# A two-layer encoder trunk on one core: the first conv block's conditioning split into scale first and shift last

## The chip, the cores and the metric

The kernel runs on one core of one Trainium2 chip. The metric is the device time in microseconds, as the median of several runs.

## The reference

The model is a trunk of two layers over x of 1024 tokens by 1024 features, in float32. Each layer normalises, modulates by a conditioning vector, mixes, and ends with a squared-ReLU MLP; layer 0 mixes with a gated short convolution, layer 1 with latent attention. The part that matters here is the entry of layer 0:

```python
c_act = silu(c)
mod = c_act @ ada_w[0] + ada_b[0]            # (1, 6 * 1024)
sh_m, sc_m, g_m, sh_f, sc_f, g_f = split(mod, 6)
h = rmsnorm(x, norm_g[0, 0]) * (1 + sc_m) + sh_m
bcx = h @ conv_in_w                          # 1024 x 3072
b_gate, c_gate, xh = split(bcx, 3)
u = c_gate * xh
conv = depthwise_conv(u, w_conv, width 3, causal) + b_conv
y = (b_gate * conv) @ w_out
x = x + g_m * rmsnorm(y, norm_g[0, 1])
```

The columns of `ada_w[0]` that belong to the shift (0 to 1023) and the scale (1024 to 2047) are 8 MB together; x is 4 MB.

## The kernel before

Every float32 operand of a product is split into a high part (rounded to the type that TensorE takes at full speed) and a low part (the difference); `mm` issues three matmuls: low by high, high by low, high by high. On the way ScalarE writes the high part and VectorE the low one (`split_w` at L163 and L164 for weights).

`conv_phase` computes the first part of layer 0. It holds h transposed, in tiles of 128 features by 512 tokens: feature tile k (0 to 7) and token half (0 or 1). In turn it

- loads conditioning columns (`ada`, tile `aw`, three buffers): for each k, 128 columns of scale and 128 of shift over all 1024 rows, 1 MB in four transfers. `ada_end` forms the product with silu(c) as an accumulation on VectorE over eight row blocks (tile `av`, L821 and L823), sums over partitions by two small matmuls with ones (L825), and makes the scale and the shift (tile `sh`, L826 and L828);
- loads x (eight row tiles `y`), normalises it (`norm_x`: square with sum and root on ScalarE, L245 and L247, reciprocal and product on VectorE, L252 and L898);
- transposes on TensorE (`turn`, L833, four transposes for a tile), and scales and shifts at the eviction (`scaled`): ScalarE writes the high part and the full value (L839), VectorE the low part (L840);
- multiplies (`products`): for each (k, half) three groups g (the c gate, the b gate, xh) of three matmuls each, 512 columns, into six accumulators in PSUM. The first column block (m = 0) goes through the sixteen (k, half) as they become ready, half 1 two steps (`LAG`) behind half 0. Then `evict(0)`, and the second column block (m = 1) over the same h. Meanwhile `sums` (L888 to L894) forms sums and differences of the quarters of h, the operands of the following column blocks;
- goes on with the remaining column blocks in pairs (`all_pairs`), a scheme of seven products for eight.

The weights of one (k, m) are 128 by 384; their raw form goes through two buffers in turn (tags acc and gmb), the split forms through a ring of four (`wr`). The order of TensorE and of the transfer queue on SyncE is pinned as written in `conv_phase`; VectorE's and ScalarE's order is left to the scheduler when the program is built. The evictions' second half (`end` in `evict`: convolution, gate, store) runs later, among the pairs.

Of the kernel before, what the change touches and what calls it, by code (L numbers as in the profile page):

```python
# [17 lines left out]
P = 128  # L18
D = 1024
S = 1024  # L20
KD = D // P
# [16 lines left out]
LAG = 2  # L38
# [11 lines left out]
def trunk_kernel(ctx: ExitStack, tc: tile.TileContext, x, c, ada_w, ada_b, norm_g, conv_in_w, conv_w,  # L50
                 conv_b, conv_out_w, kv_ada_w, kv_ada_b, kv_norm_g, kv_a_w, kv_a_norm_g, kv_b_w,
                 q_a_w, q_a_norm_g, q_b_w, attn_o_w, mlp_up_w, mlp_down_w, consts, out):
    nc = tc.nc
    uid = [0]

    def nm(s):
        uid[0] += 1
        return f"{s}_{uid[0]}"
# [4 lines left out]
    cp = pool("cp")  # L63
# [21 lines left out]
    def tp_ps():  # L85
        return ps.tile([P, HALF], F32, tag="tp", name=nm("tp"))
# [10 lines left out]
    def row_tile():  # L97
        return yp.tile([P, D], F32, tag="y", name=nm("y"), bufs=NT)
# [15 lines left out]
    def ld(out_, in_):  # L114
        nc.sync.dma_start(out_, in_)
# [32 lines left out]
    bias = cp.tile([P, BIAS_ROWS], F32, name="bias")  # L148
# [306 lines left out]
    def halves(t):  # L455
        return t[:, :HALF], t[:, HALF:]
# [307 lines left out]
    w0, w1 = ada_w[0], ada_w[1]  # L764
    x0 = x[0]

    def conv(v, u, m, lo_, hi_):

        nc.scalar.activation(v[:, lo_:hi_], u[:, lo_:hi_], AF.Identity, scale=cw[2][:, m:m + 1], bias=cb[:, m:m + 1])
        for back in (1, 2):  # L770
            o = max(lo_, back)
            nc.vector.scalar_tensor_tensor(v[:, o:hi_], u[:, o - back:hi_ - back], cw[2 - back][:, m:m + 1], v[:, o:hi_],
                                           op0=ALU.mult, op1=ALU.add)

    def conv_phase():
# [4 lines left out]
        wr = pool("wr")  # L780
# [3 lines left out]
        ops = {n: as_quarter(t_) for n, t_ in zip(("11", "21", "22"), (s11, s21, slots_of(ca, 1)[0]))}  # L784
# [20 lines left out]
        nc.vector.tensor_scalar(g1, gain(0, 0), RMS, None, op0=ALU.mult)  # L805
        nc.vector.scalar_tensor_tensor(b1, bias[:, 8:16], 1.0, g1, op0=ALU.add, op1=ALU.mult)
        sh = [cp.tile([P, 2], F32, name=nm("sh")) for _ in range(KD)]

        def ada(k):
# [8 lines left out]
        def ada_end(k, raw):  # L818
            p_ = tp_ps()
            acc = st.tile([P, 2 * P], F32, tag="av", name=nm("av"), bufs=2)  # L820
            nc.vector.tensor_scalar(acc, raw[:, 0, :], csil[:, 0:1], None, op0=ALU.mult)  # L821
            for i in range(1, KD):
                nc.vector.scalar_tensor_tensor(acc, raw[:, i, :], csil[:, i:i + 1], acc, op0=ALU.mult, op1=ALU.add)  # L823
            for j in range(2):
                nc.tensor.matmul(p_[:, j:j + 1], acc[:, j * P:(j + 1) * P], ones[:, 0:1], start=True, stop=True)  # L825
            nc.vector.scalar_tensor_tensor(sh[k][:, 0:1], p_[:, 0:1], g1[:, k:k + 1], b1[:, k:k + 1], op0=ALU.mult,  # L826
                                           op1=ALU.add)
            nc.vector.tensor_tensor(sh[k][:, 1:2], p_[:, 1:2], bias[:, k:k + 1], op=ALU.add)  # L828

        def turn(k, half):  # L830
            p_ = tp_ps()
            for t in range(4):
                nc.tensor.transpose(p_[:, t * P:(t + 1) * P], xt[half * 4 + t][:, k * P:(k + 1) * P], ident)  # L833
            return p_

        def scaled(k, p_, dst, name):
            hi, lo = ops[name][k % 4]
            for out_ in (hi, dst):
                nc.scalar.activation(out_, p_, AF.Identity, scale=sh[k][:, 0:1], bias=sh[k][:, 1:2])  # L839
            nc.vector.tensor_tensor(lo, dst, hi.bitcast(F32), op=ALU.subtract)  # L840

        def old(k):
            return kept[k % 4][:, (k // 4) * HALF:(k // 4 + 1) * HALF]

        new = [None] * 4

        def weights(k, m):

            raw = ad.tile([P, D], F32, tag=("acc", "gmb")[k % 2], name=nm("w"), bufs=1)[:, :3 * P]
            ld(raw.rearrange("p (g m) -> p g m", g=3),  # L850
               conv_in_w[0][k * P:(k + 1) * P, :].rearrange("p (g c) -> p g c", g=3)[:, :, m * P:(m + 1) * P])
            w = [wr.tile([P, 3 * P], F32R, tag="w" + part_, name=nm("w"), bufs=4) for part_ in "hl"]
            split_w(w[0], w[1], raw)
            return w

# [7 lines left out]
        def evict(m, acc):  # L863
            b, c_, u, v = (row_tile() for _ in range(4))
            for half in range(2):
                sl = slice(half * HALF, (half + 1) * HALF)
                nc.scalar.activation(c_[:, sl], acc[1, half], AF.Copy)
                nc.scalar.activation(b[:, sl], acc[0, half], AF.Copy)
                nc.vector.tensor_tensor(u[:, sl], acc[2, half], c_[:, sl], op=ALU.mult)

            def end():
                conv(v, u, m, 0, S)
                nc.vector.tensor_tensor(v, v, b, op=ALU.mult)
                nc.scalar.dma_start(hd[m], v)

            late.append(end)
# [19 lines left out]
        def norm_x(half):  # L896
            for t in range(4 * half, 4 * half + 4):
                nc.vector.tensor_scalar(xt[t], xt[t], rroot(squares(nx, xt[t])), None, op0=ALU.mult)  # L898

        def first_half(k):  # L900
            raw = ada(k)
            if k == 0:
                load_x(0)
                norm_x(0)
            elif k == LAG:
                load_x(1)
            p_ = turn(k, 0)
            ada_end(k, raw)
            scaled(k, p_, old(k), ("11", "21")[k // 4])

        def second_half(k):
            if k < 4:
                new[k] = halves(raw_tile())
            scaled(k, turn(k, 1), new[k % 4][k // 4], ("12", "22")[k // 4])

        with pinned([mybir.EngineType.PE, mybir.EngineType.SP]):
            w = [weights(0, 0)]
            first_half(0)
            acc = banks6()
            for k in range(KD + LAG):  # L920
                if k < KD - 1:
                    w.append(weights(k + 1, 0))
                    first_half(k + 1)
                if k < KD:
                    products(w[k], k, 0, acc)
                if k == LAG:
                    norm_x(1)
                    second_half(0)
                if k >= LAG:
                    if k - LAG < KD - 1:  # L930
                        second_half(k - LAG + 1)
                    products(w[k - LAG], k - LAG, 1, acc)
                if k == KD:
                    w.append(weights(0, 1))
            w = w[KD]
            st.release()
            evict(0, acc)
            cB = pool("cB", "right")
            for n, t_ in zip(("t1", "t2"), slots_of(cB, 2)):
                ops[n] = as_quarter(t_)  # L940
            ops["t3"], ops["t4"] = [], {}
            acc = banks6()
            for k in range(KD):
                w, w_ = weights(k + 1, 1) if k < KD - 1 else None, w
                products(w_, k, 0, acc)
                products(w_, k, 1, acc)
                if k % 2 == 0:
                    sums(k // 2)
            evict(1, acc)
# [130 lines left out]
    def cols_of(w, n):  # L1080
# [5 lines left out]
    up, ws, hs, firsts, _ = down_phase(slots, (2, 2, 4), conv_out_w[0], from_dram(hd), "g0m", x0, xs[0],  # L1086
                                      mlp_up_w[0], "0f")
# [93 lines left out]
    steps = h_steps(tp, ys, 0, "kv", hk[0])  # L1181
# [3 lines left out]
    steps = h_steps(tp, ys, 1, "kv", hk[1])  # L1185
# [166 lines left out]
    for h in range(H):  # L1352
# [82 lines left out]
    up, ws, hs, firsts, _ = down_phase(slots, (2, 2, 4), attn_o_w[0], from_dram(hd), "g1m", xs[1], xs[2],  # L1435
                                      mlp_up_w[1], "1f")
# [52 lines left out]
```

## Time and profile before

| | us |
|---|---|
| median of 3 runs | 2187.67 |
| lowest and highest run | 2184.27, 2188.56 |
| profiled execution, span from first to last instruction | 2182.7 |
| profiled execution's own time beside the span | not shown |
| TensorE busy in the span | 2092.2 (96%) |
| VectorE busy | 1518.3 (70%) |
| ScalarE busy | 1065.2 (49%) |
| transferred | 329.90 MB |

Everything the change touches lies in the first 160 us or so. TensorE's share there is the place to look at; from about 85 us on it is busy throughout.

### The profile page before, as it was taken

The page shows a single profiled execution, that of the slowest core. Times are in us where ns is not written, and L with a number is a line of the kernel's source. Part 1 is how long each engine was busy: PE and PEld are TensorE (multiplying, and loading weights), DVE is VectorE, ACT ScalarE, POOL GpSimd, SP SyncE. Part 2 cuts the span into 40 slices and gives each one's busy share as a digit, 9 for nine tenths or more (in the row PEclk, how much of TensorE's full clock was granted, in tenths as well). Part 3 has the DMA queues.
Part 4 walks back from the last instruction along what each step waited for, and adds up shares of the span by engine and source line. Part 5 has one row for each costly group of instructions (what it writes and reads, how often), then busy time and mean ns, then how long its engine had stood idle before and what let it go on. Part 6 is the DMA issues. An engine that isn't in the chain of part 4 may idle for free.

```text
span 2182.7 us, 25276 instructions
## 1 busy us (share of the span) xinstructions
PE 2092.2 (96%) x9654; PEld 1717.5 (79%) x9654; DVE 1518.3 (70%) x2005; ACT 1065.2 (49%) x1513; POOL 4.0 (0%) x8
## 2 busy tenths in 40 slices
PE   4999999899999999999899999999899999999998
PEld 3788888688888778888677888878688887788886
DVE  6877776876555578956788776665866665558556
ACT  4533354754444433344665555564754444444342
POOL 0000000000000000000000000000000000000000
PEclk9999999999999999999999999999999999999999
DMA  8444463256443977444224131053255553853343
GB/s 229 117 138 139 139 221 124 76 174 207 164 159 126 331 255 252 164 146 173 77 69 132 55 113 44 30 170 112 75 165 179 183 179 124 307 195 126 97 145 135
DMA packets 240111, 329.90 MB, mean 151 GB/s; under 512 B 18581, under 2 KB 141810, under 8 KB 239990
## 3 DMA queue, kind: packets, MB, share of 16 engines
q1 hardware_dynamic: 202104, 247.25, 36.0%
q10 hardware_dynamic: 37886, 81.03, 9.8%
q8 instruction: 76, 1.25, 0.2%
q14 instruction: 45, 0.37, 0.1%
HBM read 247.50 MB, written 80.74 MB: 150 GB/s over the span
## 4 chain that ended last, share of the span: by engine, by line
PE 76%; DVE 12%; ACT 6%; DMA 4%; issue 2%; ACTq 0%; SPq 0%; DVEq 0%
PE one L160 40%; PE mm L160 19%; PE tp L160 7%; PE big L160 4%; PE big L1282 2%; ACT junk L245 2%; DVE y L302 2%; DVE raw L303 2%; DMA raw<-in_ada_w_dram 1%; PE tp L1308 1%; DVE acc L185 1%; DVE y L296 1%; DMA raw<-ha 1%; DVE small L1285 1%; ACT small L247 1%
## 5 line engine op out<-in xcount | busy, mean ns | idle before, releaser
L160 PE MATMUL one<-slot,uphi 128*128 128x512 f32 x1224 | 377.4, 389 | 0.0
L160 PE MATMUL big<-slot 128*128 128x512 f32 x1152 | 267.9, 392 | 0.6 <-DVE slot L164 0.4
L160 PEld LDWEIGHTS one<-slot,uphi 128*128 128x128 f32 x1224 | 230.1, 188 | 48.2 <-issue 0.5
L160 PEld LDWEIGHTS big<-slot 128*128 128x128 f32 x1152 | 216.0, 188 | 46.1 <-ACT y L746 1.0
L164 DVE TENSOR_TENSOR uplo<-raw,uphi 128x1024 fp32r<-128x1024 f32 x127 | 153.0, 1221 | 137.0 <-ACT uphi L163 136.9
L160 PE MATMUL one<-slot,uplo 128*128 128x512 f32 x612 | 240.3, 393 | 5.9 <-ACT y L564 2.3
L160 PE MATMUL one<-ring,ring 128*128 128x512 f32 x1008 | 233.6, 392 | 6.8 <-DVE ring L164 6.8
L163 ACT ACTIVATE ring<-w 128x1024 fp32r<-128x1024 f32 x98 | 103.7, 1059 | 262.9 <-PE tp L160 131.5
L160 PEld LDWEIGHTS one<-ring,ring 128*128 128x128 f32 x1008 | 189.5, 189 | 49.8 <-ACT ring L163 5.6
L163 ACT ACTIVATE uphi<-raw 128x1024 fp32r<-128x1024 f32 x127 | 134.5, 1061 | 128.6 <-PE one L160 88.7
L164 DVE TENSOR_TENSOR ring<-w,ring 128x1024 fp32r<-128x1024 f32 x98 | 119.7, 1221 | 109.7 <-ACT ring L163 109.6
L160 PE MATMUL mm<-slot,uphi 128*128 128x512 f32 x520 | 165.0, 398 | 9.7 <-DVE slot L363 9.3
L160 PE MATMUL mm<-ring,ring 128*128 128x512 f32 x672 | 162.4, 390 | 0.0
L160 PE MATMUL tp<-ring,ring 128*128 128x512 f32 x672 | 161.7, 389 | 0.0
L185 DVE SCALAR_TENSOR_TENSOR acc<-raw,csil,acc 128x1024 f32<-128x1024 f32 x88 | 112.8, 1281 | 49.8 <-DMA raw<-in_ada_w_dram 46.4
L160 PEld LDWEIGHTS mm<-ring,ring 128*128 128x128 f32 x672 | 125.7, 188 | 27.1 <-DVE ring L164 0.6
L160 PEld LDWEIGHTS tp<-ring,ring 128*128 128x128 f32 x672 | 126.2, 188 | 26.2
L160 PEld LDWEIGHTS one<-slot,uplo 128*128 128x128 f32 x612 | 115.1, 188 | 33.0 <-ACT y L489 3.7
L164 DVE TENSOR_TENSOR ring<-raw,ring 128x1024 fp32r<-128x1024 f32 x98 | 119.3, 1218 | 18.2 <-ACT ring L163 18.2
L160 PEld LDWEIGHTS mm<-slot,uphi 128*128 128x128 f32 x520 | 97.4, 189 | 33.3 <-DVE slot L363 10.8
L489 ACT ACTIVATE y<-one 128x512 f32<-128x512 f32 x66 | 39.0, 590 | 169.3 <-PE one L160 93.2
L160 PE MATMUL one<-slot,s 128*128 128x512 f32 x468 | 112.6, 389 | 0.5 <-DVE s L164 0.5
(255 smaller groups left out, 3474.4 us busy)
## 6 DMA issues: line engine op xcount, KB each, us to landing
ha<-y ACTq DMA_DIRECT2D x196, 256.0 KB, 3.9
raw<-ha SPq DMA_DIRECT2D x98, 512.0 KB, 3.9
raw<-in_ada_w_dram SPq DMA_DIRECT2D x80, 512.0 KB, 4.3
raw<-in_mlp_up_w_dram SPq DMA_DIRECT2D x70, 512.0 KB, 4.3
w<-in_mlp_down_w_dram SPq DMA_DIRECT2D x56, 512.0 KB, 5.3
raw<-hd SPq DMA_DIRECT2D x24, 512.0 KB, 4.5
xs<-raw ACTq DMA_DIRECT2D x24, 512.0 KB, 3.4
raw<-xs SPq DMA_DIRECT2D x24, 512.0 KB, 3.3
```

The source lines that it names most:

```text
L160: nc.tensor.matmul(out_, lhs[a], rhs[b], start=first and i == 0, stop=last and i == 2, skip_group_check=more)
L163: nc.scalar.activation(hi, src, AF.Copy)
L164: nc.vector.tensor_tensor(lo, src, hi.bitcast(F32), op=ALU.subtract)
L185: nc.vector.scalar_tensor_tensor(acc, raw, s, acc, op0=ALU.mult, op1=ALU.add)
L245: nc.scalar.activation(junk, src, AF.Square, accum_out=ss)
L247: nc.scalar.activation(rt, ss, AF.Sqrt, bias=eps_d)
L296: nc.vector.tensor_tensor(y, y, p_, op=ALU.add)
L302: nc.vector.scalar_tensor_tensor(y, y, rroot(ss), self.gmb, op0=ALU.mult, op1=ALU.mult)
L303: nc.vector.tensor_tensor(xr, xr, y, op=ALU.add)
L489: nc.scalar.activation(dst, x_, AF.Copy)
L1282: nc.tensor.matmul(o_, a, m_, start=j == 0, stop=j == 4 and b * HALF + w < n)
L1285: nc.vector.tensor_reduce(mx, sp[:, :n], AX.X, ALU.max, negate=True)
```

## The change

Scale and shift are loaded apart: `ada(col, q)` takes 256 columns of one of them, for the feature tiles 2q and 2q+1, in two transfers. The four scale tiles come first; the four shift tiles follow. `scaled` makes h without the shift, and the first column block (three feature tiles of the result: b, c and xh for m = 0) is computed from it. When a shift has come (`shift_end`), `shifted` adds it to the four h tiles in place: two ScalarE operations and one difference on VectorE for each. The shift's share in the first column block is computed by `bias_products`: for each k and group two matmuls (high and low weights) with the shift's high and low part as two columns, 48 in all, 36 after the first block and 12 after the first product pair of the second. The share (`add`, three numbers for each feature) is added in the later part of `evict`. The sixteen products of the first block follow a written list of steps; the ring of split weights has ten buffers instead of four, so that the first block's weights stay.

```diff
+        def ada(col, q):
             raw = st.tile([P, KD, 2 * P], F32, tag="aw", name=nm("aw"), bufs=3)
             for i in (0, 4):
-                for j, col in enumerate((D, 0)):
-                    ld(raw[:, i:i + 4, j * P:(j + 1) * P],
-                       w0[i * P:(i + 4) * P, col + k * P:col + (k + 1) * P].rearrange("(k p) m -> p k m", p=P))
+                ld(raw[:, i:i + 4, :],
+                   w0[i * P:(i + 4) * P, col + 2 * q * P:col + 2 * (q + 1) * P].rearrange("(k p) m -> p k m", p=P))
             return raw
...
+        def scale_end(q, raw):
+            pr = slice(2 * q, 2 * q + 2)
+            sc[q] = cp.tile([P, 2], F32, name=nm("sc"))
+            nc.vector.tensor_tensor(sc[q], ada_end(raw), g1[:, pr], op=ALU.mult)
+            nc.vector.tensor_tensor(sc[q], sc[q], b1[:, pr], op=ALU.add)
+
+        def shift_end(q, raw):
+            sh[q] = cp.tile([P, 2], F32, name=nm("sh"))
+            nc.vector.tensor_tensor(sh[q], ada_end(raw), bias[:, 2 * q:2 * q + 2], op=ALU.add)
+            shr[q] = cp.tile([P, 2, 2], F32R, name=nm("shr"))
+            nc.vector.tensor_copy(shr[q][:, :, 0], sh[q])
+            nc.vector.tensor_tensor(shr[q][:, :, 1], sh[q], shr[q][:, :, 0].bitcast(F32), op=ALU.subtract)
+            for half in range(2):
+                for k in (2 * q, 2 * q + 1):
+                    shifted(k, half)
...
+        def scaled(k, half, p_):
+            f, (hi, lo) = place(k, half)
+            for out_ in (hi, f):
+                nc.scalar.activation(out_, p_, AF.Copy, scale=sc[k // 2][:, k % 2:k % 2 + 1])
+            nc.vector.tensor_tensor(lo, f, hi.bitcast(F32), op=ALU.subtract)
+
+        def shifted(k, half):
+            f, (hi, lo) = place(k, half)
+            for out_ in (hi, f):
+                nc.scalar.activation(out_, f, AF.Identity, bias=sh[k // 2][:, k % 2:k % 2 + 1])
+            nc.vector.tensor_tensor(lo, f, hi.bitcast(F32), op=ALU.subtract)
...
-            w = [wr.tile([P, 3 * P], F32R, tag="w" + part_, name=nm("w"), bufs=4) for part_ in "hl"]
+            w = [wr.tile([P, 3 * P], F32R, tag="w" + part_, name=nm("w"), bufs=10) for part_ in "hl"]
...
+        def bias_products(ws_, ks, out_):
+            for k in ks:
+                for g in range(3):
+                    for q in ws_[k]:
+                        nc.tensor.matmul(out_[:, 2 * g:2 * g + 2], q[:, g * P:(g + 1) * P], shr[k // 2][:, k % 2, :],
+                                         start=k == 0 and g == 0 and q is ws_[k][0],
+                                         stop=k == KD - 1 and q is ws_[k][1], skip_group_check=True)
+
+        def evict(m, acc, add=None):
...
+                if add is None:
+                    nc.vector.tensor_tensor(u[:, sl], acc[2, half], c_[:, sl], op=ALU.mult)
+                else:
+                    nc.vector.tensor_copy(u[:, sl], acc[2, half])
             def end():
+                v = row_tile()
+                if add is not None:
+                    nc.scalar.activation(u, u, AF.Identity, bias=add[:, 2:3])
+                    nc.vector.scalar_tensor_tensor(u, c_, add[:, 1:2], u, op0=ALU.add, op1=ALU.mult)
                 conv(v, u, m, 0, S)
+                    nc.vector.scalar_tensor_tensor(v, b, add[:, 0:1], v, op0=ALU.add, op1=ALU.mult)
...
+            w = [weights(0, 0)]
+            aw = [ada(D, 0)]
+            load_x(0)
+            norm_x(0)
+            w.append(weights(1, 0))
+            scale_end(0, aw.pop())
+            acc = banks6()
+            steps = [(k, 0) for k in range(4)] + [(0, 1), (1, 1), (4, 0), (2, 1), (3, 1), (5, 0), (4, 1), (6, 0), (5, 1),
+                                                  (7, 0), (6, 1), (7, 1)]
+            ready(*steps[0])
+            for i, (k, half) in enumerate(steps):
+                if i == 0:
+                    aw.append(ada(D, 1))
+                    w += [weights(j, 0) for j in (2, 3)]
+                    load_x(1)
+                elif i == 1:
+                    scale_end(1, aw.pop())
+                    norm_x(1)
+                    aw.append(ada(D, 2))
+                    w += [weights(j, 0) for j in (4, 5)]
+                elif i == 3:
+                    aw.append(ada(D, 3))
+                    w += [weights(j, 0) for j in (6, 7)]
+                elif i == 4:
+                    scale_end(2, aw.pop(0))
+                    aw.append(ada(0, 0))
+                elif i == 8:
+                    scale_end(3, aw.pop(0))
+                    aw += [ada(0, 1), ada(0, 2)]
+                elif i == 12:
+                    shift_end(0, aw.pop(0))
+                    aw.append(ada(0, 3))
+                elif i == 14:
+                    shift_end(1, aw.pop(0))
+                if i + 1 < len(steps):
+                    ready(*steps[i + 1])
+                products(w[k], k, half, acc)
+            shift_end(2, aw.pop(0))
+            bsum = tp_ps()
+            wn = [weights(j, 1) for j in range(2)]
+            bias_products(w, range(6), bsum)
+            shift_end(3, aw.pop(0))
+            add = cp.tile([P, 3], F32, name="add")
+            evict(0, acc, add)
...
             for k in range(KD):
+                products(wn[k], k, 0, acc)
+                products(wn[k], k, 1, acc)
+                if k == 0:
+                    bias_products(w, range(6, KD), bsum)
+                    nc.vector.tensor_reduce(add, bsum[:, :6].rearrange("p (g two) -> p g two", two=2), AX.X, ALU.add)
+                if k + 2 < KD:
+                    wn.append(weights(k + 2, 1))
                 if k % 2 == 0:
                     sums(k // 2)
```

In the changed program some lines have other numbers: the small matmuls that end a sum are L824, the scaling is L858 and L859, the shifting in place L865 and L866, the shift's share L894.

More of the change, by code (lines that the diff above doesn't have):

```diff
@@ L834, in turn, with place @@
             return p_
[L836 to L840, printed above, removed]
+        def place(k, half):
+            f = new[k % 4][k // 4] if half else old(k)
+            return f, ops[("1", "2")[k // 4] + ("1", "2")[half]][k % 4]
+        def scaled(k, half, p_):
[8 more added lines that the diff above has]
+            nc.vector.tensor_tensor(lo, f, hi.bitcast(F32), op=ALU.subtract)
         def old(k):
@@ L898, in norm_x, with ready @@
                 nc.vector.tensor_scalar(xt[t], xt[t], rroot(squares(nx, xt[t])), None, op0=ALU.mult)
[L900 to L912, printed above, removed]
+        def ready(k, half):
+            if half and k < 4:
@@ L913, in second_half @@
                 new[k] = halves(raw_tile())
-            scaled(k, turn(k, 1), new[k % 4][k // 4], ("12", "22")[k // 4])
+            scaled(k, half, turn(k, half))
         with pinned([mybir.EngineType.PE, mybir.EngineType.SP]):
             w = [weights(0, 0)]
-            first_half(0)
-            acc = banks6()
[L920 to L926, printed above, removed]
-                    norm_x(1)
[L928 to L934, printed above, removed]
```

22 lines of the change are left out of this document (7 added, 15 removed).

## The prediction

> **What bounds the kernel now.** I read the page's slices first, then the waits of TensorE in the first 130 us, then the timeline there, then busy time by stretches.
>
> ```profile
> PE   4999999899999999999899999999899999999998
> PE tp L825 <- DVE av L823: 10.6, 4, 6.9
> PE tp L833 <- DVE y L898: 6.2, 4, 2.3
> ```
>
> The row of tenths has one digit for each fortieth of the span, 54.6 us; the wait rows give us in total, times, longest. From the second slice on TensorE is at 8 or 9 tenths; the first stands at 4. The two wait rows say what is late: TensorE's small matmuls that end the conditioning sums (L825) wait for VectorE's accumulation (10.6 us in 4 waits), and the transposes wait for normalised x.
>
> ```profile
> 24.99 2.91 PE L160 MATMUL mm<-slot,w 128*128 128x512 f32 x6
> 69.13 0.58 PE L825 MATMUL tp<-ones,av 128*128 128x1 f32 x4 [1.39 <-DVE av L823]
> 69.57 2.58 PE L160 MATMUL mm<-slot,w 128*128 128x512 f32 x6
> 85.61 1.52 PE L160 MATMUL mm<-slot,w 128*128 128x512 f32 x6
> 118.25 0.39 PE L160 MATMUL one<-slot,uplo 128*128 128x512 f32 x1
> ```
> ```profile
> 69.10:73.50 4.40, 4.37 (x15) 3.48 (x16) 1.32 (x4) 1.45 (x2) 0.00 (x0) 0.61 0.16 45
> 85.40:118.20 32.80, 32.80 (x146) 27.20 (x145) 29.30 (x44) 15.77 (x27) 0.96 (x1) 1.00 0.55 168
> ```
>
> The first product starts at 24.99, the sixteen products of the first column block end at about 85.4, those of the second block end at 118.25 and the paired blocks start there. From 85.4 on TensorE never waits (32.80 busy of 32.80, but VectorE has 29.30 beside it, so only 3.5 us of room). So the change can gain before 85.4 only, and a delay at 118.25 is carried to the end, because TensorE is full after it. In the rows of stretches the third number from the end is the granted clock: after a gap of 1.39 us the granted clock fell to 0.61 for 4.4 us.
>
> **Prices used.**
>
> ```profile
> 91.21 2.72 PE one L160 x12
> 55.04 0.60 PE L833 MATMUL tp<-cs,y 128*128 128x128 f32 x4
> 49.98 0.50 PE L825 MATMUL tp<-ones,av 128*128 128x1 f32 x4
> 46.05 0.77 ACT L839 ACTIVATE raw<-tp,sh 128x512 f32<-128x512 f32 x1
> 46.71 0.78 ACT L839 ACTIVATE b<-tp,sh 128x512 fp32r<-128x512 f32 x1
> 88.98 1.65 ACT L892 ACTIVATE slot<-raw 128x512 fp32r<-128x512 f32 x3
> 92.87 0.68 DVE L891 TENSOR_TENSOR raw<-raw 128x512 f32<-128x512 f32 x1
> 93.47 0.68 DVE L894 TENSOR_TENSOR slot<-raw,slot 128x512 fp32r<-128x512 f32 x1
> ```
> ```profile
> L823 DVE SCALAR_TENSOR_TENSOR av<-aw,csil,av 128x256 f32<-128x256 f32 x56 | 26.6, 481 | 1.0
> L245 ACT ACTIVATE junk<-y 128x1024 bf16<-128x1024 f32 x8 | 8.4, 1046 | 2.4 <-DMA y<-in_x_dram 2.4
> L247 ACT ACTIVATE small<-small,eps_d 128x1 f32<-128x1 f32 x8 | 2.3, 291 | 0.2
> L898 DVE TENSOR_SCALAR y<-y,small 128x1024 f32<-128x1024 f32 x8 | 6.0, 750 | 0.1
> L164 DVE TENSOR_TENSOR w<-w,w 128x384 fp32r<-128x384 f32 x16 | 8.8, 552 | 1.7 <-ACT w L163 1.7
> L164 DVE TENSOR_TENSOR uplo<-raw,uphi 128x1024 fp32r<-128x1024 f32 x3 | 3.7, 1222 | 1.1 <-ACT uphi L163 1.1
> L163 ACT ACTIVATE uphi<-raw 128x1024 fp32r<-128x1024 f32 x3 | 3.2, 1063 | 5.8 <-DVE raw L445 2.1 <-DVE raw L438 2.0 <-DMA raw<-in_conv_in_w_dram 1.6
> ```
>
> A 512-column matmul takes 2.72/12 = 0.227 us, a product (nine of them) 2.04; at the low clock (24.99: six in 2.7) 0.458 and 4.1. A turn (four transposes) is 0.6, an end of a conditioning sum 0.5 (about 1.0 at the low clock). Two ScalarE operations with a bias follow each other after 0.66 us, plain copies after 0.52; VectorE's 512-column operations after 0.60. An accumulation step is 0.48.
>
> **The change part by part.** Of the changed program I use the order in which its instructions stand on each engine; engines work theirs off in that order.
>
> *Loads and sums.* The bytes are the same, eight conditioning tiles of 1 MB. VectorE's sums stay 8 x (1 + 7) steps; but four sums, not eight, stand ahead of the products, two columns each. The first scale now stands ahead of the normalisation of x, on VectorE too, which waits about 1 us for the small matmul: x tile 3 is normalised at an estimated 20.4 instead of
>
> ```profile
> 18.84 0.75 DVE L898 TENSOR_SCALAR y<-y,small 128x1024 f32<-128x1024 f32 x1
> ```
>
> (19.6). But no second sum stands before the first product: after the last transpose (0.5), two scaled copies (1.4) and the difference (0.7) it starts at 23.1, 1.9 us earlier than 24.99.
>
> *From there to the first shift (twelve products).* Work: 12 x 2.04 + 11 turns x 0.6 + 4 sums' ends x 0.5 = 33.1. Two waits remain. (a) The turn of the second half of x stands before the fourth product. ScalarE has, from the third turn on (28.4: 23.1 + eight matmuls at 0.458, a sum's end 0.9 and the turn 0.7 at the low clock), two scaled tiles (2.8), two squares with the read-out of their sums (2 x 1.2) and three roots (0.9), 6.1 us, then VectorE 1.5 (reciprocal, one sum step, norm): 36.0, and TensorE is there at 33.3: 2.9 us with the dispatch. (b) The third scale's sum: VectorE from 36.1 has four weight splits (2.1), eight interleaved steps and one difference, done at 42.1; TensorE is there at 40.7: 1.4 us. Each gap is as long as the 1.39 us gap above or longer, so I count a low clock after each and at the start, 2 us lost each time (nine matmuls at 0.458 instead of 0.227). 23.1 + 33.1 + 2.9 + 1.4 + 6 = 66.5. Before, ten products were done by then; here twelve. So far the change gains about 5 us.
>
> *The shifts.* This is where I expect it to lose. Each shift end issues eight ScalarE operations (two for each of four tiles) and four differences on VectorE, and on ScalarE they stand like this:
>
> ```
> L865 Activation slot_3_161<-q_10_168,sh_122_616 (eight of L865 here)
> L858 Activation slot_4_162<-tp_127_648 (scaled tile 7, first half)
> L858 Activation slot_5_163<-tp_133_711 (scaled tile 7, second half, hi)
> L865 Activation slot_3_161<-q_12_170,sh_129_682 (eight of L865 here)
> L858 Activation raw_111_509<-tp_133_711 (scaled tile 7, second half, full)
> ```
>
> The shifts of tiles 0 to 3 thus stand ahead of the scaling of tile 7, for which the products wait. No row of before has a bias alone from SBUF; between 0.52 and 0.66 I take 0.66, the biased operation's. First shift: from the end of its sum at 66.5, 0.4 (small VectorE step) + 8 x 0.66 + 2 scaled (1.4) + difference 0.7 = 7.8; TensorE has a turn, a product, a turn (3.2) meanwhile: a wait of 4.5. Product (7, first) runs on at 74.3, eight matmuls at the low clock 3.7: 78.0. Second shift: sum's end and turn 1.7, hi 0.7, 8 x 0.66 = 5.3, full 0.7, difference 0.7 = 9.1; TensorE has 3.8 meanwhile: a wait of 5.3. The last product goes on at 87.1 and ends, again low, at 90.8: 5.4 us later than 85.4. With 0.52 it is 2.2 less.
>
> *The shift's share in the products.* 48 matmuls of two columns, each with its own weights; nearest row: 4 in 0.50 us. 36 of them and two sums' ends stand between the blocks: 36 x 0.13 + 1.0 = 5.7, with a third of a us for the wait on the third shift 6.0; nothing else is queued for TensorE, so all of it counts (from 4.5, if weights load at 0.1, to 10, at the low clock's 1.0 in four). The other 12 stand behind the second block's first product pair: 1.6. They could be free only if TensorE waited there anyway; it doesn't.
>
> *Second block.* VectorE here gets differences of two shifts (8 x 0.60) besides the sums of the paired operands (32 x 0.60) and the splits. Its add-up of the shift's share stands ahead of ten such operations and then the split of the third weights; it waits for the twelve small matmuls, 5.7 us after the block's start, then 0.2 + 10 x 0.60 + 0.55: 12.4. TensorE is there at 9.8: 2.6 us. After that VectorE keeps ahead.
>
> *Start of the pairs.* Before, the first paired weights' low part was split 20 us ahead:
>
> ```profile
> 97.55 1.22 DVE L164 TENSOR_TENSOR uplo<-raw,uphi 128x1024 fp32r<-128x1024 f32 x1
> ```
>
> Now the high part stands behind ScalarE's four evictions of the block, and the low part behind VectorE's two: from the end of the second-last group (0.7 before the block's end) 0.6 + 1.06 + 1.22, a wait of 2.3. What else the eviction's new end adds (one ScalarE operation of 1024 and one VectorE one, about 1.1 and 1.3) lies in the pairs, where VectorE idles; cost 0, at most 2.4 if that cover were gone.
>
> *The clock at these two gaps.* Nearest row: 1.39 us of gap cost 2 us; 0.9 us of gap,
>
> ```profile
> 47.60 2.11 PE L160 MATMUL one<-b,w 128*128 128x512 f32 x8 [0.89 <-DVE b L840]
> ```
>
> cost nothing (8 in 1.9 us). 2.6 and 2.3 lie beyond the first: 1.9 each, between 0 and 3.8 for both. The Trainium skill, page "TensorE: Matmul & The Clock Gate", section "Why this matters for your kernels", says that the clock falls for idle gaps above about 3 us between bursts; by that these two would be free and the sum 3.8 less. The trace's 1.39 us gap disagrees, so I follow the row.
>
> **The sum.** 5.4 + 6.0 + 1.6 + 2.6 + 2.3 + 3.8 = 21.7 us. Against the profiled execution's span of 2182.7 that gives 2204.4. No execution time other than the span is shown for it; the median of the runs, 2187.67, is 5.0 above it, so I predict 2187.7 + 21.7 = 2209.4.
>
> **Rivals.**
> 1. *Faster: the shifts hide.* The point from which it decides is whether scaling tile 7 waits on ScalarE. If shifts cost the path nothing (because their data came early, or ScalarE was far ahead), the block ends at 66.5 + 0.5 + 3 x 0.6 + 4 x 2.04 = 77.0, 8.4 before 85.4; and if gaps (a) and (b) with their clock go too (2.9 + 1.4 + 4 = 8.3), 16.7 is gained, 7.6 paid for the small matmuls: 9.1 faster, 2178.6. For it: the waits of 10.6 and 6.2 us that before has. Against: the order above, in which nothing lets ScalarE pass. Chance 0.10.
> 2. *No difference.* The shifts hide, gaps (a) and (b) stay: 8.4 gained, 7.6 paid, 2186.9. The same rows speak for it and against it. Chance 0.07.
> 3. *Slower by half.* The shift's operations go at 0.52, the small matmuls at 0.1, and the clock does not fall at the two late gaps: 21.7 - 2.2 - 1.8 - 3.8 = 13.9, 2201.6; with one early gap less (4) 10. Part of my case; chance 0.30.
> 4. *Loads late.* The queue on SyncE waits for weight buffers ahead of the conditioning tiles (the seventh weights wait for the fifth's split, at 36.7). If the shift tiles land some 5 us late, the shift ends move by that: 26.7, 2214. Chance 0.10.
> Forecast as summed: 0.43.
>
> **How the numbers follow.** The measurement tells 0.2% (4.4 us) from no change. Slower: cases 3, 4 and the forecast, 0.83; same 0.07; faster 0.10. The range leaves out rivals 1 and 2 and the ends of the rest: from half-way below case 3's 10 us (2195) to the late loads and small matmuls at the low clock (2215).
>
> **What would show it.** Right: in the profile after, TensorE has waits of 4 to 5 us on differences of the last two products (L859), behind eight ScalarE operations of L865; 36 matmuls of L894 at about 0.13 us; the first product at about 23; a wait on a weight split at the second block's third tile; one for the low part at the start of the pairs, at about 140 instead of 118. Wrong: a second block that starts before 85, a TensorE that does not wait in the last four products, or shifts that lie in ScalarE's idle time.

## The result, and the profile after

| | us |
|---|---|
| before, in the same session: median of 4 runs | 2185.97 (2179.99 to 2188.56) |
| after: median of 4 runs | 2219.07 (2216.85 to 2220.6) |
| ratio after to before, 95% interval | 1.0156 (1.0142 to 1.0171) |
| profiled execution, span before and after | 2182.7 and 2218.8 |

The change makes the kernel 33 us slower. The forecast was 21.7 us slower; 2219.07 lies above its range, which ended at 2215.

First the waits of TensorE in the first 160 us after the change that bear on the change (us in total, times, longest), then its timeline there (start, us, what; the wait before it and who ended it in brackets):

```profile
PE tp L847 <- DVE y L944: 6.0, 5, 1.8
PE one L160 <- DVE slot L859: 4.6, 1, 4.6
PE tp L824 <- DVE av L822: 4.6, 2, 3.3
PE mm L160 <- ACT slot L858: 2.8, 1, 2.8
PE mm L160 <- DVE w L164: 2.4, 1, 2.4
```
```profile
40.10 0.98 PE L824 MATMUL tp<-ones,av 128*128 128x1 f32 x4 [3.28 <-DVE av L822]
70.67 0.79 PE L160 MATMUL mm<-slot,w 128*128 128x512 f32 x1 [2.83 <-ACT slot L858]
84.41 3.64 PE L160 MATMUL one<-slot,w 128*128 128x512 f32 x8 [4.58 <-DVE slot L859]
88.25 5.18 PE L894 MATMUL tp<-shr,w 128*128 128x2 f32 x36
94.14 2.91 PE L160 MATMUL mm<-slot,w 128*128 128x512 f32 x6
108.31 2.93 PE L160 MATMUL mm<-slot,w 128*128 128x512 f32 x6 [2.44 <-DVE w L164]
137.42 0.50 PE L160 MATMUL one<-slot,uplo 128*128 128x512 f32 x1 [2.19 <-DVE uplo L164]
```

Every wait that the prediction named is there. The second block starts at 94.14 instead of 85.61, the pairs at 137.42 instead of 118.25: 19.2 us lost by then, where the prediction's terms gave 19.8 (21.7 less the clock behind the pairs' start). So the first 137 us hold the waits that were written down, and nearly their sum. That the sum came so close is partly luck: the second block starts 8.5 us late where 11.4 were forecast, and loses 10.6 more where 8.4 were. But the end comes 36.1 us later in the two spans; some 17 us were lost after the place where the prediction stopped looking. No new wait is large enough for them. Most are in the matmuls themselves. One tile's matmuls (ns of one: least, median, most), before and then after:

```profile
L160 PE MATMUL one<-q,uphi x328: 387/389/628, 140.2 to 1859.5; 128*128 128x512 f32 x164
L160 PE MATMUL mm<-slot,qw x180: 387/389/476, 1165.2 to 1408.1; 128*128 128x512 f32 x180
L160 PE MATMUL one<-b,uphi x72: 387/389/397, 126.6 to 287.3; 128*128 128x512 f32 x72
```
```profile
L160 PE MATMUL one<-q,uphi x328: 392/397/628, 161.4 to 1894.6; 128*128 128x512 f32 x164
L160 PE MATMUL mm<-slot,qw x180: 391/397/481, 1196.8 to 1439.8; 128*128 128x512 f32 x180
L160 PE MATMUL one<-b,uphi x72: 387/389/397, 147.6 to 312.2; 128*128 128x512 f32 x72
```

The work is the same, its shapes too, and none of it is code that the diff touches. Yet most of the matmuls that take one operand from q and the other from uphi last 397 ns instead of 389, and those of b and uphi don't. What differs is where the tiles lie. In SBUF, the memory from which TensorE takes its operands, one group of pools (each pool holds the buffers of some tiles) grows from the low end (there the small tiles, raw, y, q, part of the slots), another from the high end (uphi, uplo, b, ring). The change puts 13 small tiles of 32 bytes per partition (`sc`, `sh`, `shr`, `add`) where before had 8 (`sh`): all low tiles behind them lie 160 bytes further, while the high ones stay. In before a low and a high big tile begin at the same place modulo 256; after, they don't.

### The profile page after: what moved, and what is told of

Read it like the earlier page. It is cut to its first block, busy times and chain, and to the rows that moved or that the text cites. A ratio compares the mean times of both kernels' runs of the same rounds, so it can differ in the third digit from the quotient of the medians.

```text
span 2218.8 us, 25384 instructions
## 1 busy us (share of the span) xinstructions
PE 2125.8 (96%) x9702; PEld 1733.2 (78%) x9702; DVE 1530.1 (69%) x2027; ACT 1084.1 (49%) x1546; POOL 4.0 (0%) x8
## 4 chain that ended last, share of the span: by engine, by line
PE 74%; DVE 12%; ACT 6%; DMA 5%; issue 2%; ACTq 0%; SPq 0%; DVEq 0%
PE one L160 38%; PE mm L160 20%; PE tp L160 7%; PE big L160 4%; DMA raw<-in_ada_w_dram 3%; PE big L1345 2%; ACT junk L245 2%; DVE y L302 2%; DVE raw L303 2%; DVE acc L185 1%; PE tp L1371 1%; DVE y L296 1%; DMA raw<-ha 1%; DVE small L1348 1%; ACT small L247 1%
## 5 line engine op out<-in xcount | busy, mean ns | idle before, releaser
L160 PE MATMUL one<-slot,uphi 128*128 128x512 f32 x1224 | 383.3, 394 | 0.0
```

The lines of the kernel that those rows point to most:

```text
L160: nc.tensor.matmul(out_, lhs[a], rhs[b], start=first and i == 0, stop=last and i == 2, skip_group_check=more)
```

## Experiments

**Where the tiles lie.** Eight kernels add nothing but unused tiles; seven of them add a single one, among the small tiles.

```diff
-    cp.tile([P, 8], F32, name="even")
+    cp.tile([P, 8], F32, name="even"); cp.tile([P, N], F32, name="pad")   # N floats of padding
```

a_pad is the changed kernel with N = 8 (32 bytes; the low tiles then lie 192 bytes from where before has them). b_32 and b_64 are the kernel before with 32 and 64 bytes. b_both, the one with two, is before with 32 bytes below and 32 above, so that low and high tiles move towards each other by 32 each:

```diff
+    rp = pool("rp", "right"); rp.tile([P, 8], F32, name="padr")
```

> The changed kernel with one more small tile (32 bytes a partition) in the pool of small tiles, so that the tiles allocated after it on that side start 32 bytes past a multiple of 64 as in the kernel before, not at a multiple of 64 as in the changed kernel. Theory A (the small tiles of the change moved the big ones, and TensorE reads from there more slowly: about 1900 more matmuls at 230 to 238 ns instead of 227 after the first 140 us): about 14 us faster than the changed kernel, near 2205, pitch back at 227 ns. Theory B (something else slows the matmuls: the run, the chip's state, the code's place): no difference, near 2219.

> The kernel before with the same 32-byte tile: its big tiles on that side now start at multiples of 64. Nothing else differs. Theory A: about 15 us slower than before, near 2202, the matmuls that take an operand from these tiles at 230 to 238 ns. Theory B: no difference, near 2187.

> The kernel before with 64 bytes more instead of 32. Theory A (what counts is the place within 64 bytes): no difference. If any move of the tiles slows them: 15 us slower like the 32 bytes.

> The kernel before with 32 bytes more on both sides of the memory, so that all big tiles start at multiples of 64. Theory A1 (the two operands of a matmul, one from each side, must lie alike within 64 bytes): no difference from before. Theory A2 (a place at a multiple of 64 is slow by itself): slower than with 32 bytes on one side, 20 us or more over before, since operands of both sides suffer, with 227 ns nowhere.

Measured: a_pad 2214.16 (1.0134 of before), b_32 2197.23 (1.0059, 1.0047 to 1.0072), b_64 2194.16 (1.0043, 1.003 to 1.0055), b_both 2195.36 (1.0044, 1.0032 to 1.0056). So an unused tile of 32 bytes costs the unchanged kernel 13 us, and the theory that it is a tile's place within 64 bytes falls: 64 bytes cost nearly as much, and a_pad gains 5 us on the changed kernel instead of the 14 expected. b_both, in which the distance of low and high tiles changes by 64 as in b_64, costs as much as b_64: it looks like the distance of the two operands. The rows of its profile say so too (b_32 first, then b_both):

```profile
L160 PE MATMUL one<-q,uphi x328: 389/396/628, 142.6 to 1872.2; 128*128 128x512 f32 x164
```
```profile
L160 PE MATMUL one<-q,uphi x328: 388/392/628, 142.0 to 1871.1; 128*128 128x512 f32 x164
L160 PE MATMUL one<-b,uphi x72: 387/389/548, 128.3 to 291.9; 128*128 128x512 f32 x72
```

q lies at the same place in both kernels, and its matmuls go from 396 to 392 ns when uphi moves; 392 is also what b_64 has (below). And uphi isn't slow by its own new place: with b, which moved along with it, it stays at 389. So it is the distance. Then at what period?

> The kernel before with 512 bytes of padding: nothing of its work changes. Theory M with a modulus of 512 or less: as before, ratio 1.000. With a modulus of 1024: slower by about 10 us (1.004 to 1.006), as with 32 or 64 bytes. Rival X: slower likewise.

> The kernel before with 256 bytes of padding. Theory M with a modulus of 256 or less (128 would do too): as before, ratio 1.000. With a modulus of 512 or 1024: slower by about 10 us (1.004 to 1.006). Rival X: slower likewise. Together with the 512 bytes it places the modulus.

> The kernel before with 128 bytes of padding. 256 and 512 bytes cost nothing, 32 and 64 about 10 us. If the period of the operands' distance is 128 bytes or less: ratio 1.000. If it is 256: slower by about 10 us, 1.004 to 1.006.

Measured: 512 bytes 1.0013 (1.0004 to 1.0022), 256 bytes 1.0001 (0.9992 to 1.001), 128 bytes 1.0042 (1.0029 to 1.0056). The same tile's matmuls in b_64, b_128 and b_256:

```profile
L160 PE MATMUL one<-q,uphi x328: 388/392/628, 139.7 to 1865.5; 128*128 128x512 f32 x164
```
```profile
L160 PE MATMUL one<-q,uphi x328: 387/395/628, 140.4 to 1869.1; 128*128 128x512 f32 x164
```
```profile
L160 PE MATMUL one<-q,uphi x328: 388/389/629, 139.5 to 1858.9; 128*128 128x512 f32 x164
```

At 256 the median is back at 389. TensorE's busy time in the profiles agrees: 2092.2 us in before, 2108.0, 2101.4 and 2102.7 with 32, 64 and 128 bytes, 2104.7 in b_both, and 2090.7 and 2093.1 with 256 and 512. So of the distances tried, the multiples of 256 bytes cost TensorE nothing to speak of and the others 9 to 16 us; the 2.8 us by which b_512 is slower as a whole, at the edge of its interval, are not explained. Last, the cure on the changed kernel itself, N = 216, which with the 160 bytes makes 1024:

> The changed kernel with 864 bytes of padding beside its small tiles, so that its left-side tiles stand 1024 bytes per partition further than in the kernel before (instead of 160) and are congruent with the right-side ones modulo 1024 again, as there. Theory M (what slows the matmuls is the distance of the two operands' tiles modulo 1024 or a divisor of it): matmuls of left with right operands go at 227 ns again, the stretches of 50 us in the pairs hold 222 to 223 matmuls, and the time falls by about 14 us from the changed kernel's, to about 2205 (ratio to before 1.009). Rival X (any move of the left tiles slows, whatever its size, for example because they come nearer to the right ones or cross some absolute border): the slow matmuls stay, about 2214 to 2219 (1.013 to 1.015). Waits of the first 140 us as in the changed kernel on either.

Measured: 2208.61 (1.0116, 1.0102 to 1.013). First the engines' busy row and then the tile's row, of the changed kernel and then of a_1024:

```profile
PE 2125.8 (96%) x9702; PEld 1733.2 (78%) x9702; DVE 1530.1 (69%) x2027; ACT 1084.1 (49%) x1546; POOL 4.0 (0%) x8
```
```profile
PE 2111.9 (96%) x9702; PEld 1734.7 (79%) x9702; DVE 1529.5 (69%) x2027; ACT 1084.0 (49%) x1546; POOL 4.0 (0%) x8
L160 PE MATMUL one<-q,uphi x328: 388/389/629, 161.6 to 1882.7; 128*128 128x512 f32 x164
```

The same 9702 matmuls take 13.9 us less of TensorE at the same mean granted clock (0.986 and 0.985), and the time falls by 10.5 us by the medians, 8.7 by the ratios. Behind the start of the pairs, the changed kernel loses 16.9 us of its span against before and a_1024 3.4. That is the missing part: placed like before, the change costs 25.0 us, 3 more than the prediction's sum.

**The shifts ahead of tile 7.** c_late is a_1024 with the shifting taken out of the shift's end and written behind the last product; the first block's eviction moves up with it:

```diff
+        def shift_in(q):
             for half in range(2):
                 for k in (2 * q, 2 * q + 1):
                     shifted(k, half)
...
                 products(w[k], k, half, acc)
+            shift_in(0)
+            add = cp.tile([P, 3], F32, name="add")
+            evict(0, acc, add)
             shift_end(2, aw.pop(0))
+            shift_in(1)
...
             bias_products(w, range(6), bsum)
+            shift_in(2)
             shift_end(3, aw.pop(0))
-            add = cp.tile([P, 3], F32, name="add")
-            evict(0, acc, add)
+            shift_in(3)
```

> The changed kernel with 864 bytes of padding as in a_1024, and with the shifting in place taken out of the shift's end and written behind the last product of the first block (sums of the shift stay where they are), so that ScalarE scales tile 7 ahead of all shifts. Theory S (the waits of 2.8 and 4.6 us at tile 7 and the low clock after them come from the eight shifts ahead on ScalarE, the prediction's step): these two waits go, the first block ends 8 to 11 us earlier than in a_1024 (near 75 to 77 instead of 85), and the whole is 5 to 10 us faster than a_1024, the lower end if the shifts that are now later make the second block wait. Rival D (the sums of the shift on VectorE, or the differences, are late anyway): the waits stay within 2 us, and the time within 3 us of a_1024.

Measured: 2192.15 (1.0042, 1.003 to 1.0055), 16.5 us faster than a_1024, more than expected. The timeline of TensorE in c_late:

```profile
69.63 4.62 PE L160 MATMUL one<-slot,w 128*128 128x512 f32 x18
74.45 4.58 PE L896 MATMUL tp<-shr,w 128*128 128x2 f32 x36
79.75 2.91 PE L160 MATMUL mm<-slot,w 128*128 128x512 f32 x6
95.06 2.92 PE L160 MATMUL mm<-slot,w 128*128 128x512 f32 x6 [3.10 <-DVE w L164]
123.63 0.50 PE L160 MATMUL one<-slot,uplo 128*128 128x512 f32 x1 [2.21 <-DVE uplo L164]
```

The last eighteen matmuls of the first block run without a gap and end at 74.2, not at 88 as after; both waits are gone, and the low clock behind them. Theory S holds: the eight operations on ScalarE ahead of tile 7 were the largest term.

**The shift's share.** n_share is a_1024 without the 48 small matmuls (the share is left out of the first block's result, `add` is zero):

```diff
-            bias_products(w, range(6), bsum)
...
-                    bias_products(w, range(6, KD), bsum)
-                    nc.vector.tensor_reduce(add, bsum[:, :6].rearrange("p (g two) -> p g two", two=2), AX.X, ALU.add)
+                    nc.vector.memset(add, 0.0)
```

> a_1024 without the 48 small matmuls: the shift's share in the first column block is left out (its three numbers are set to zero), so the first block's outputs lack it; all else stays. Theory T (the prediction's term: 6.0 us between the blocks and 1.6 us behind the second block's first pair, all on the path, and the clock low behind them): the second block starts 5 to 6 us earlier, the third tile's weights are waited for no longer (no step on VectorE waits for the twelve small matmuls), so the whole is 8 to 12 us faster than a_1024, near 2198. Rival W (TensorE then waits for the shift's sums or the shifted operands instead): less than 4 us gained, with new waits of some us on a sum (L824) or on a difference.

Measured: 2195.26 (1.005, 1.0035 to 1.0066), 13.4 us less than a_1024 by the medians, 9.8 by the two profiled spans, where 8 to 12 were expected. In a_1024 the 36 matmuls ran at the low clock (granted 0.50, against 0.79 in the profile after) and took 7.82 us, not 5.18. But one expectation of the text fell. TensorE of n_share, then its VectorE:

```profile
88.93 1.65 PE L160 MATMUL mm<-slot,w 128*128 128x512 f32 x6
101.76 2.93 PE L160 MATMUL mm<-slot,w 128*128 128x512 f32 x6 [4.37 <-DVE w L164]
```
```profile
90.23 1.29 DVE L914 SCALAR_TENSOR_TENSOR y<-y,add,y 128x1024 f32<-128x1024 f32 x1 [0.56 <-ACT y L913]
94.52 0.69 DVE L866 TENSOR_TENSOR slot<-raw,slot 128x512 fp32r<-128x512 f32 x1 [1.14 <-ACT raw L865]
101.15 0.56 DVE L164 TENSOR_TENSOR w<-w,w 128x384 fp32r<-128x384 f32 x1
```

Without the add-up the third tile's weights are waited for all the more, 4.37 us instead of 2.50. Their split stands on VectorE behind the differences of the shifts, which wait for ScalarE, and here also behind the adding of the (zero) share (L914), which comes this early only because the share is ready at once. In a_1024 VectorE does what the prediction says: it idles until the small matmuls are done, adds up, does ten operations and then splits:

```profile
103.80 0.17 DVE L1007 TENSOR_REDUCE add<-tp 128x3 f32<-128x6 f32 x1 [4.74 <-PE tp L894]
109.90 0.55 DVE L164 TENSOR_TENSOR w<-w,w 128x384 fp32r<-128x384 f32 x1
```

Counted from the start of the second block (96.52 and 88.93), the split is done after 13.9 us in a_1024 and after 12.8 in n_share, while TensorE is there after 11.5 and 8.5. So the add-up is in the path, but the rest of that queue is late enough without it; how much of the 2.50 us is the add-up's own is not told apart.

**The second block.** f_ring is c_late with weights loaded three tiles ahead, the last twelve small matmuls behind the third product pair, and two rings for the split weights:

```diff
-            w = [wr.tile([P, 3 * P], F32R, tag="w" + part_, name=nm("w"), bufs=10) for part_ in "hl"]
+            w = [(wq, wr)[m == 0].tile([P, 3 * P], F32R, tag="w" + part_, name=nm("w"), bufs=(4, 8)[m == 0]) for part_ in "hl"]
...
-                if k == 0:
+                if k == 2:
                     bias_products(w, range(6, KD), bsum)
...
-                if k + 2 < KD:
-                    wn.append(weights(k + 2, 1))
+                if k + 3 < KD:
+                    wn.append(weights(k + 3, 1))
```

> c_late with three edits around the second block: the split weights of the two blocks go through two rings (eight and four buffers) instead of one of ten, so that the first paired weights' place in SBUF overlaps no weights still in use; weights are loaded three tiles ahead instead of two; the last twelve small matmuls and the add-up stand behind the third product pair instead of the first. Theory R (the wait of 2.2 us at the start of the pairs comes from the ring of ten lying where the paired weights go, and the wait of 3.1 us from the add-up ahead of the weight split on VectorE): both waits and the low clock behind them go, the pairs start at about 116 to 118 instead of 123.6, and the whole is 7 to 10 us faster than c_late, near 2183 to 2185. Rival V (VectorE is full in the second block, so that whatever is taken from one wait comes back at the next): waits of about the same sum stay in the second block or in the first pair, and under 4 us are gained.

f_all adds to that: the share as 16 wide matmuls inside the second block (three small ones then turn the sum), the fourth shift's sum behind that block's first pair, the third scale's sum one step later, and 96 bytes of padding, so that the low tiles lie 256 bytes from where before has them:

```diff
+            for k in range(KD):
+                for i, q in enumerate(ws_[k]):
+                    nc.tensor.matmul(out_[0:2, :3 * P], shr[k // 2][:, k % 2, :], q, start=k == 0 and i == 0,
+                                     stop=k == KD - 1 and i == 1, skip_group_check=True)
...
-                elif i == 4:
+                elif i == 5:
                     scale_end(2, aw.pop(0))
```

> f_ring, and the shift's share in 16 wide matmuls (the shift's two parts as stationary operand, 384 columns of weights moving) inside the second block with three small ones to turn the sum, instead of 48 small ones; the third scale's sum one step later (ahead of the turn of tile 4 instead of the turn of (1, second)); padding so that the left tiles are congruent with before modulo 256. If the parts add up: 36 small matmuls (4.6 us) and the low clock after them go for 16 x 0.17 + 0.5 = 3.2 us of wide ones, 3 to 4 us gained; the wait of 3.3 us on the third sum goes to about 0.5 with its clock, 4 us gained: near 2176, faster than before (ratio 0.995 to 0.998). Rival V: VectorE, full through the second block, makes TensorE wait for shifted operands at its start or for the sums of the operands at the pairs: 2181 to 2187, no difference from before.

Measured: f_ring 2188.76 (1.0021, 1.0012 to 1.003), f_all 2183.86 (0.9995, 0.9986 to 1.0003), which is the time of before. TensorE in f_ring, then in f_all:

```profile
114.89 0.39 PE L160 MATMUL one<-slot,uplo 128*128 128x512 f32 x1
123.33 4.54 PE L160 MATMUL one<-slot,s 128*128 128x512 f32 x12 [2.84 <-DVE s L164]
```
```profile
71.42 1.63 PE L160 MATMUL mm<-slot,w 128*128 128x512 f32 x6
89.30 2.95 PE L896 MATMUL tp<-w,shr 128*2 128x384 f32 x16
110.38 0.47 PE L160 MATMUL one<-slot,uplo 128*128 128x512 f32 x1 [0.52 <-DVE uplo L164]
119.40 4.38 PE L160 MATMUL one<-slot,s 128*128 128x512 f32 x12 [3.29 <-DVE s L164]
277.12 1.84 PE L204 MATMUL mm<-ones,acc 128*128 128x1 f32 x16
279.78 4.34 PE L160 MATMUL one<-slot,s 128*128 128x512 f32 x12 [0.82 <-DVE s L164]
387.06 1.32 PE L338 MATMUL tp<-cs,y 128*128 128x128 f32 x8 [0.97 <-ACT q L339]
```

In f_ring both waits go and the pairs start at 114.89, 8.7 us earlier than in c_late; which of the three edits did it isn't told apart. But 8 us on, a new wait of 2.84 us with its low clock takes half of that back: rival V is right in that VectorE passes its lateness on, only later than I thought. Of the whole time 3.4 us are gained on c_late by the medians, 2.9 by the spans and 4.6 by the ratios. f_all shows the same twice over. It starts the pairs 7.9 us ahead of before (110.38 against 118.25). The wait at 119.40 and its low clock take 5.4 of that: at 277.12 f_all is 2.5 us ahead of before. Then it waits 0.82 us where before waits 0.50, its clock falls behind that (twelve matmuls in 4.34 us instead of 3.02), and the last half us goes to a wait of 0.57 us at 307.76, which before doesn't have. By 387 f_all stands where before stands:

```profile
279.62 1.84 PE L204 MATMUL mm<-ones,acc 128*128 128x1 f32 x16
281.96 3.02 PE L160 MATMUL one<-slot,s 128*128 128x512 f32 x12 [0.50 <-DVE s L164]
387.07 1.33 PE L338 MATMUL tp<-cs,y 128*128 128x128 f32 x8 [0.97 <-ACT q L339]
```

In both kernels the chain of waits between 250 and 282 runs through transfers of conditioning columns and their sums on VectorE. That stream is not a fixed limit: its transfers begin at 257.77, 262.77 and 268.58 in f_all and at 260.26, 265.31 and 270.68 in before, so it comes earlier when TensorE does and takes back only 0.3 of the 2.5 us. What takes the first stage's gain is the two waits with the low clock behind them, and at the end a transfer of `hd` (in the chains at 300.60 and 301.12), which ends at 305.7 in both kernels. That is read from the profiles; no run moved these waits.

## Why the prediction was wrong

**The step that failed** is one that it did not have: "From 85.4 on TensorE never waits ... TensorE is full after it", from which it followed that a delay at 118.25 is carried to the end and nothing is added. The delay was carried, but behind it the untouched matmuls took longer, by the place of the tiles. The prediction put that term at nothing without a reason; it is 13.9 us of TensorE's time and 8.7 to 10.5 us of the kernel's. Rows of before could not show it, because there the low and the high tiles lie well to one another; the built program's list of tiles, which moved by 160 bytes, could have raised the question.

The reading was too wide as well: its rows end at 118.2. Behind 118.25 TensorE in before is busy for 2003.8 of 2063.8 us, so it does wait, for some 60 us, and what is won at the pairs' start can be lost again in such waits, as f_all shows.

**The terms that it had**, against the profile after:

- First product at 23.1: its first matmul began at 21.81, the others, which need the difference, at 23.12.
- (a), second half of x, 2.9 us: the waits on y together are those of the transposes at the start too; the one meant was 1.85. (b), third scale's sum, 1.4: it was 3.28. The mechanisms were right, the sizes of the two off in opposite directions, 4.3 forecast and 5.1 measured. In f_all, where that sum stands one step later, it isn't waited for. Of the three low clocks counted here one did not come: behind the 1.85 us six matmuls took 1.63.
- Shifts ahead of tile 7, 4.5 and 5.3: measured 2.83 and 0.51 (high part, then difference) and 4.58. The six biased operations from 66.28 to 69.95 took 0.61 us each, between the 0.52 and the 0.66 of the prediction. ScalarE at the first shift:

```profile
65.03 1.34 ACT L865 ACTIVATE slot<-q,sh 128x512 fp32r<-128x512 f32 x2 [1.34 <-DVE sh L836]
66.28 1.32 ACT L865 ACTIVATE q<-q,sh 128x512 f32<-128x512 f32 x2
69.95 0.67 ACT L858 ACTIVATE slot<-tp,sc 128x512 fp32r<-128x512 f32 x1
```

- Small matmuls, 6.0 and 1.6: the 36 took 5.18 (0.14 each), with the two sums' ends 6.2 from 87.89 to 94.14; the 12 took 1.4. So the second block starts 8.5 us late against 11.4 forecast; but behind the small matmuls the clock was low (six matmuls in 2.91 us at 94.14 instead of 1.52), for which the sum had nothing.
- Weight split at the third tile, 2.6: 2.44. Right in size, and a_1024 has the path that was written (add-up, ten operations, split); but n_share shows that the wait does not hang on the add-up alone.
- Start of the pairs, 2.3 (its own terms add up to 2.2): 2.19.
- The clock at these two gaps, 3.8: the six matmuls behind the first took 2.93 us instead of 1.52. Behind the second the low clock came too, but not in a_pad, a_1024, c_late or n_share, with the same gap of 2.2. The price itself came from one of two outcomes: before has a gap of 1.39 us at 69.13 and six matmuls in 2.58 us behind it, but in b_64 and b_128, which do the same work, the same gap (1.37 and 1.38) is followed by six in 1.63.

**The rivals.** Rival 1 (the shifts hide) and 2 fell: the waits are there. c_late shows that they were a matter of order: written later, the shifts do hide, and the first block ends 11 us before that of before. Even so rival 1's gain of 9 us did not come, since the gain is taken away later. Rival 3 expected no low clock at the late gaps; at the first it came in each of the five profiles that have that gap (after, a_pad, a_1024, c_late, n_share). Rival 4: VectorE, which sums the conditioning columns, waits for their loads only at 7.43 and 10.23, on the first scale; no shift tile came late.

**The size of the rest.** In a_1024 the pairs start at 139.00, 20.8 us later than before. About 2 of the other 4 us come at 303.71, where a wait that before had at 281.96 with 0.50 is 0.88 and the clock falls behind it (twelve matmuls in 4.53 instead of 3.02):

```profile
303.71 4.53 PE L160 MATMUL one<-slot,s 128*128 128x512 f32 x12 [0.88 <-DVE s L164]
```

## What to carry to other kernels

Before costing an edit, list which tiles its new buffers move, not only which instructions it adds: here 160 bytes of small tiles were between a quarter and a third of the whole loss, far from the edited code, and padding to a multiple of 256 took it back. When a span grows and no wait grows with it, compare the durations of untouched instructions by operand pair. Work that a later stage will need can still hurt an earlier one by its place in an engine's queue; write it behind what is due first, and then follow the time gained through the later waits to see whether it reaches the end.

## What the runs showed of the hardware

- A matmul of 128x512 whose two operands come from tiles at different places modulo 256 bytes took up to 397 ns by its median instead of 389; pads of 32, 64 and 128 bytes cost the whole kernel 12.9, 9.4 and 9.2 us by their ratios, 256 cost nothing that can be told from none. That it is the distance of the operands and not each one's own place is shown by the rows of b_both; what in the memory has this period stays open.
- In the first 140 us of the profiles the clock fell after every gap of 2.44 us and above, but gaps of 1.4, 1.85 and 2.2 us were followed by it in some runs only: six matmuls behind the 1.85 us gap took 1.63 us in c_late and 2.91 us in f_all. A gap of half a us behind sixteen one-column matmuls (L204) had both outcomes too: twelve matmuls in 3.02 us at 281.96 in before (gap 0.50), in 4.61 us at 305.27 in the profile after (gap 0.52). Behind the 1.85 us gap, c_late and then f_all:

```profile
34.32 1.63 PE L160 MATMUL mm<-slot,w 128*128 128x512 f32 x6
```
```profile
35.56 2.91 PE L160 MATMUL mm<-slot,w 128*128 128x512 f32 x6
```

The Trainium skill, page "TensorE: Matmul & The Clock Gate", section "What's actually happening", has the clock set by windows of about 3.4 us that run freely. A window that begins at another moment in each run agrees with one gap having both outcomes; no run here shows the windows themselves.
- Matmuls of two columns, though TensorE is busy with them, were followed by the low clock as a gap is: in c_late, where eighteen full matmuls without a gap stand ahead of the 36, the six full ones behind them took 2.91 us at 79.75 (granted clock 0.50 from 78.9 to 83.0), against 1.63 at 71.42 in f_all, which has none there.
